# A hybrid two-layer trunk on one core: other buffers, engines and a fixed order for the first chunk

## The chip, the cores and the metric

The kernel runs on one core of one Trainium2 chip. The metric is the device time of one execution in microseconds (us), as the median of several runs of the same program. Five engines work side by side, each through its own list of instructions in order: TensorE (PE; its weight loads are shown apart as PEld), VectorE (DVE), ScalarE (ACT), GpSimd (POOL) and SyncE (SP, which here only starts transfers). They wait for one another through semaphores.

## The reference, cut to what matters

All of it is in float32, for 256 tokens of width 1024. A first layer mixes a state-space scan with gated linear attention, a second one is attention; each starts with an RMS norm and ends with a projection that is added to x.

```python
def rms_norm(x, w):
    x32 = x.astype(jnp.float32)
    y = x32 * lax.rsqrt(jnp.mean(x32 * x32, axis=-1, keepdims=True) + RMS_EPS)
    return y * w.astype(jnp.float32)

def ssd_gla_layer(x, norm_w, w_in, ...):
    h = rms_norm(x, norm_w)
    u = h @ w_in.astype(jnp.float32)
    z_a, xbc, dt_raw, q_b, k_b, v_b, gate_lr, g_b = split_cols(u, EVEN_SPLITS)
    ...
    out = jnp.concatenate([y_a, o_b], axis=-1) @ w_out.astype(jnp.float32)
    return x + out.astype(x.dtype)

def reference(x, ...):
    x = ssd_gla_layer(x, ...)
    x = moba_layer(x, ...)
    return rms_norm(x, final_norm).astype(x.dtype)
```

Only the very first part matters here: x times its norm weights goes into the first products at once, and the sum of squares of x, from which the norm's factor comes, is applied to the products afterwards.

## The kernel before, in words

**Products.** Each float32 operand is split into a high part (`float32r`) and the rest: `h_...` and `l_...` for weights, `hhi` and `hlo` for x. A product is three matmuls (high by high, high by low, low by high: `mm3`, line 158 is the matmul). ScalarE makes a weight's high part (line 78), VectorE the low part (line 79), both in `split`.

**Weight pieces.** Weights come from HBM as a list of pieces, in the order of use: eight pieces of the first token-major chunk (`a0_0` to `a0_7`, 128x416, one for each of the 8 row blocks of x), then `b_8` and `b_9` (128x1024 each, feature-major blocks), then `a1_0` to `a1_3` (128x832), `b_0` and so on. A piece lands in one of the 4 buffers of the pool `wraw`, and such a buffer is free again when its piece has been split. High and low parts have 7 buffers each. `need(piece)` asks for a piece and splits up to four pieces ahead of it.

**The first chunk.** `CUTS_A0` gives the transfers on SP's queue in pairs: row block k of x (`xT`, 128x256, line 186) and piece `a0_k` (line 72). Each block of x is then scaled by its norm weights into `hhi` (even blocks on VectorE, line 214; odd ones on ScalarE, line 212) and `hlo` (VectorE, line 215). TensorE runs 20 warm-up matmuls on zeros (`warmp`, line 176) and then 6 matmuls for each of the 8 blocks into `pa0_0` and `pa0_1`; then come the 24 matmuls of the block `pb8`, of `pb9`, and then of chunk a1.

**The squares of x.** `xsq` is x squared, in four pairs of row blocks: two pairs on GpSimd (line 224), two on ScalarE (line 222). Four additions on GpSimd (line 226) bring the eight blocks down to one. TensorE then sums over the partitions with a matmul on ones (`ss1`), which stands in its list after the 15th matmul of `pb8`. From `ss1` come `rcol_v` (VectorE) and `rcol` (GpSimd, a power), with which all products of the layer are scaled.

**Order.** TensorE's list is written out in program order (`manual_schedule`), with the small products of the mixers put between those of the projections after given delays (`DL`). The lists of the other engines are ordered by the scheduler. SP starts a transfer when the buffer is free and when the transfer that used the same one of 8 transfer semaphores has landed.

Of the kernel before, what the change touches and what calls it, by code (L numbers as in the profile page):

```python
# [9 lines left out]
F32 = mybir.dt.float32  # L10
F32R = mybir.dt.float32r
AF = mybir.ActivationFunctionType
ALU = mybir.AluOpType
AX = mybir.AxisListType

P = 128
T = 256
D = 1024
KB = D // P
# [1 line left out]
NEG = -1e30  # L21
NW = 7
NWARM = 20
# first weight pieces: (first row block, number of them)
CUTS_A0 = tuple((k, 1) for k in range(8))
AHEAD = 4
# tensor-engine time (ns) left to the other engines between the steps of a mixer
DL = {"ss": 1350, "rb": 5000, "gt": 1500, "ac": 7300, "act": 2600, "lg": 2150, "ln": 2250, "cb": 12400,
      "pair0": 11900, "pair1": 9700, "gla0": 650, "glagap": 3650, "gla1": 3350, "gla2": 8700, "r2": 10000,
      "turn": 4150, "rb1": 4000, "at0": 2600, "at2": 4350, "at3": 1800, "gqk": 250}  # L30
# feature-major blocks of the first projection: 0-9 convolved, 10-13 q, 14-17 k, 18-25 gate
# a1-a4: chunks of the token-major columns
ORDER_A = (8, 9, "a1", 0, 10, 1, 11, 2, 14, 3, 13, 5, 12, 4, 15, 16, 6, "a3", 7, 17, "a2", "a4")
GLA_NEEDS = ("a3", "a3", "a4", "a4")

# columns of the packed constants
C_EN, C_SN, C_ON = 0, 8, 16
C_CW, C_CB, C_GB, C_DS, C_GN = 24, 64, 74, 78, 86
C_DTB, C_AL = 87, 103
C_N = 119  # L40
# columns of the packed matrices of shape
M_ID, M_TRI, M_MASK, M_SEL = 0, 128, 384, 768
M_N = 784

# [2 lines left out]
def trunk(ctx, tc, xT_d, x_d, cst_d, mat_d, gw2_d, fn_d, wa_d, wb_d, wc_d, wv_d, wp_d, wf_d, out_d):  # L47
    nc = tc.nc
    V, S, G, TE = nc.vector, nc.scalar, nc.gpsimd, nc.tensor
# [5 lines left out]
    big = ctx.enter_context(tc.tile_pool(name="big", bufs=1))  # L55
# [7 lines left out]
    def pg(name):  # L63
        return psg.tile([P, 512], F32, name=name, tag="g")
# [1 line left out]
    def pm(name):  # L66
        return psm.tile([P, 512], F32, name=name, tag="m")

    # ------------------------------------------------------------------ weights
    def fetch(src, kbs, cols, name):  # L70
        raw = wraw.tile([P, kbs, cols], F32, name="r_" + name, tag="raw")
        nc.sync.dma_start(raw, src)
        return raw

    def split(raw, kbs, cols, name):
        hi = whi.tile([P, kbs, cols], F32R, name="h_" + name, tag="hi")
        lo = wlo.tile([P, kbs, cols], F32R, name="l_" + name, tag="lo")
        S.activation(hi, raw, AF.Copy)  # L78
        V.tensor_sub(lo, raw, hi.bitcast(F32))  # L79
        return hi, lo  # L80

    pieces, index, got, raws = [], {}, [], []
# [5 lines left out]
    def prefetch(end):  # L88
        for j in range(len(got), min(len(pieces), end)):
            k_, src, kbs, cols = pieces[j]  # L90
            name = "_".join(str(q_) for q_ in k_)
            if j >= len(raws):
                raws.append(fetch(src, kbs, cols, name))
            got.append(split(raws[j], kbs, cols, name))

    def need(key, oldest=None):
        i = index[key]
        prefetch(max(i + 1, min(i + AHEAD, index[oldest or key] + NW)))
        return got[i]
# [22 lines left out]
    for n in range(2):  # L122
        plan_tm(f"f{n}", wf_d[n])

    # ------------------------------------------------------------------ order of the tensor engine
    # The projections are the main stream; the mixers are generators that run beside it.
    # A generator yields the tensor-engine time (ns) after which its next step may be queued.
    clock = {"now": 0.0, "seq": 0}
    waiting = []

# [34 lines left out]
    def mm3(ps, ahi, alo, bhi, blo, first, last):  # L165
        mm(ps, ahi, bhi, first, False)
        mm(ps, ahi, blo, False, False)
        mm(ps, alo, bhi, False, last)
        due()

    # keep the tensor engine's clock up until the first operands arrive
    warm = cpool.tile([P, T], F32R, name="warm")
    V.memset(warm.bitcast(F32), 0.0)
    wps = pm("warmp")
    for _ in range(NWARM):
        TE.matmul(wps[:, 0:T], warm[:, 0:P], warm, start=True, stop=True)

    # ------------------------------------------------------------------ inputs
    xT = big.tile([P, KB, T], F32, name="xT", tag="xT")
    cst = cpool.tile([P, C_N], F32, name="cst")  # L180
    mat = cpool.tile([P, M_N], F32, name="mat")
    gw2 = cpool.tile([16, 512], F32, name="gw2")
    nc.scalar.dma_start(cst, cst_d)
    j = 0
    for k0, n_ in CUTS_A0:
        nc.sync.dma_start(xT[:, k0:k0 + n_, :], xT_d[:, k0:k0 + n_, :])
        for k_, src, kbs, cols in pieces[j:j + (1 if j < len(CUTS_A0) - 1 else 3)]:
            raws.append(fetch(src, kbs, cols, "_".join(str(q_) for q_ in k_)))
        j += 1
    nc.sync.dma_start(mat, mat_d)  # L190
    nc.sync.dma_start(gw2, gw2_d)

    ident = mat[:, M_ID:M_ID + P]
# [10 lines left out]
    hhi = big.tile([P, KB, T], F32R, name="hhi", tag="hhi")  # L204
    hlo = big.tile([P, KB, T], F32R, name="hlo", tag="hlo")
    xsq = big.tile([P, KB, T], F32, name="xsq", tag="y")
    kb = 0
    for i, n_ in enumerate(n_ for _, n_ in CUTS_A0):
        for kb in range(kb, kb + n_):
            en = cst[:, C_EN + kb:C_EN + kb + 1]  # L210
            if kb % 2:
                S.activation(hhi[:, kb, :], xT[:, kb, :], AF.Copy, scale=en)
            else:
                V.tensor_scalar(hhi[:, kb, :], xT[:, kb, :], en, None, op0=ALU.mult)
            V.scalar_tensor_tensor(hlo[:, kb, :], xT[:, kb, :], en, hhi[:, kb, :].bitcast(F32),  # L215
                                   op0=ALU.mult, op1=ALU.subtract)
        kb += 1
        prefetch(i + 1)
    for k4 in range(4):
        sq, src = xsq[:, 2 * k4:2 * k4 + 2, :], xT[:, 2 * k4:2 * k4 + 2, :]  # L220
        if k4 % 2:
            S.activation(sq, src, AF.Square)
        else:
            G.tensor_tensor(sq, src, src, op=ALU.mult)
    for a, b, n_ in ((0, 2, 2), (4, 6, 2), (0, 4, 2), (0, 1, 1)):
        G.tensor_tensor(xsq[:, a:a + n_, :], xsq[:, a:a + n_, :], xsq[:, b:b + n_, :], op=ALU.add)

    def rms_from_sum(ss, n, width, name):
        v = sm.tile([P, n], F32, name=name + "_v", tag=name + "_v")
# [18 lines left out]
    rhalf, rsq, rsv, rsh = (cpool.tile([P, 2], F32, name=n_) for n_ in ("rhalf", "rsq", "rsv", "rsh"))  # L248
    env = {}

    # ------------------------------------------------------------------ even in-projection
    v = big.tile([P, 2, D], F32, name="v", tag="v")
    gs = big.tile([P, 2, D], F32, name="gs", tag="gs")
    dtr = sm.tile([P, 2, 16], F32, name="dtr", tag="dtr", bufs=1)
# [17 lines left out]
            V.scalar_tensor_tensor(gs[:, tt, glo:ghi], th[:, 0:n], 1.0, src, op0=ALU.add, op1=ALU.mult)  # L272

    def gemm_tm(name, hi8, lo8, cols, outs, cuts=((0, 2), (2, 2), (4, 2), (6, 2))):
        """Token-major product of both token tiles, a weight piece at a time."""
        for q_, (k0, n_) in enumerate(cuts):
            hi, lo = need((name, k0 if name == "a0" else q_))
            for tt in range(2):
                for j in range(n_):
                    kb = k0 + j  # L280
                    mm3(outs[tt][:, 0:cols], hi8[:, kb, tt * P:tt * P + P], lo8[:, kb, tt * P:tt * P + P],
                        hi[:, j, :], lo[:, j, :], kb == 0, kb == KB - 1)

    def gemm_a(c):
        ps = [pg(f"pa{c}_{tt}") for tt in range(2)]
        cuts = CUTS_A0 if c == 0 else ((0, 2), (2, 2), (4, 2), (6, 2))
        gemm_tm(f"a{c}", hhi, hlo, 416, ps, cuts)
        return ps
# [28 lines left out]
    def co_first(ps):  # L317
# [9 lines left out]
        yield DL["rb"]  # L327
        S.activation(rb, row_bcast([rcol[:, tt:tt + 1] for tt in range(2)], "rbp")[:, 0:T], AF.Copy)
        env["rb"] = True
        # softplus of the step sizes, by the series of artanh  # L330
        V.scalar_tensor_tensor(na, dtr, -1.0, dtr, op0=ALU.mult, op1=ALU.min)
        S.activation(se, na, AF.Exp)
        V.tensor_scalar(sd, se, 2.0, None, op0=ALU.add)
# [25 lines left out]
        for tt in range(2):  # L359
            TE.transpose(act[:, 16 * tt:16 * tt + 16], acT[:, tt * P:tt * P + P], ident[0:16, 0:16])  # L360
        V.tensor_copy(acs, act[:, 0:32].rearrange("p (a b) -> p a b", a=2))
        # gate logits -> cumulated log decay (times 16)
        for b2 in range(2):
            lg = pm(f"lg{b2}")
            for j in range(2):
                b = 2 * b2 + j
                mm(lg[:, j * T:j * T + T], gw2[:, b * P:b * P + P], glT)
            for j in range(2):
                b = 2 * b2 + j
# [8 lines left out]
        V.tensor_tensor_scan(flat(gcs), flat(scanm), flat(gmn), 0.0, op0=ALU.mult, op1=ALU.add)  # L378
        env["gcs"] = True

    # convolution and silu
    xs = big.tile([P, KB, T], F32, name="xs", tag="xT")
    bc = big.tile([P, 2, T], F32, name="bc", tag="bc")
    pads = []
# [68 lines left out]
        V.scalar_tensor_tensor(y[:, blk, :], xs[:, blk, :], cst[:, C_DS + blk:C_DS + blk + 1], yp[:, 0:T],  # L453
                               op0=ALU.mult, op1=ALU.add)

    # gated linear attention
    q = big.tile([P, 4, T], F32, name="q", tag="obhi")
    k = big.tile([P, 4, T], F32, name="k", tag="oblo")
    f3 = lambda a: a.rearrange("p a (c d) -> p (a c) d", d=64)
# [120 lines left out]
            if env["nqk"] == 8:  # L580
                spawn(co_gla_qk())

    # ------------------------------------------------------------------ gate of the state-space half
    x1 = big.tile([P, 2, D], F32, name="x1", tag="xT")
    nc.scalar.dma_start(x1, x_d)
    ylate = {}
# [22 lines left out]
    for b in range(KB):  # L609
# [3 lines left out]
                               op0=ALU.mult, op1=ALU.subtract)  # L613
# [4 lines left out]

    spawn(co_r2())

    # ------------------------------------------------------------------ even out-projection
    for n in range(2):
        ps = [pg(f"pc1_{n}_{tt}") for tt in range(2)]
        gemm_tm(f"c1{n}", obhi, oblo, 512, ps)
# [8 lines left out]
                kb == 0, kb == KB - 1)  # L633

    def gemm_tt(name, hi8, lo8, tag):
        """Token-major product, one token tile after the other: yields each when it is done."""
        for tt in range(2):
            ps = pg(f"{tag}{tt}")
            part(ps, name, hi8, lo8, tt, range(KB), (name, 0) if tt == 0 else None)
            yield tt, ps  # L640
# [39 lines left out]
            due()  # L680
    spawn(co_norm())

    # ------------------------------------------------------------------ second layer
    va = big.tile([P, 2, D], F32, name="va", tag="y")
    for n in range(2):
        for tt, ps in gemm_tt(f"v{n}", h1hi, h1lo, f"pv{n}"):
# [52 lines left out]
    for pr in range(8):  # L739
        qk = []  # L740
        for i in range(2):
            ps = gemm_fm(("p", 3 * pr + i), h1hi, h1lo, f"pp{pr}_{i}")
            t_ = tmp.tile([P, T], F32, name=f"qk{pr}_{i}", tag=("t1a", "t1c")[i])
            n_ = (P, T)[i]
# [18 lines left out]
        V.scalar_tensor_tensor(zs, th, 1.0, zs, op0=ALU.add, op1=ALU.mult)  # L763
        env[("z", pr)] = zs

    # ------------------------------------------------------------------ last projection and norm
    fnb = big.tile([P, D], F32, name="fnb", tag="s2")
    nc.scalar.dma_start(fnb, fn_d.to_broadcast([P, D]))
    ssf = sm.tile([P, 2, 3], F32, name="ssf", tag="ssf", bufs=1)
# [122 lines left out]
```

## Time and profile before

| | before |
|---|---|
| median of 3 runs | 349.83 us |
| fastest and slowest run | 348.47 and 350.31 us |
| span of the profiled execution | 347.5 us |
| PE busy | 335.5 us, 97% |
| DVE, ACT, POOL busy | 263.5, 217.5 and 49.3 us |

The span goes from the first to the last instruction of the profiled execution. The page gives that execution no own time beside its span; the three timed runs lie 1.0 to 2.8 us above the span. PE's busy time is modelled (matmuls overlap), so its pace is read from the distance between starts.

### The profile page before, as it was taken

How to read it: one execution, taken by the hardware profiler on the slowest of the kernel's cores; microseconds unless marked ns; L12 is line 12 of the kernel's file. 1: busy time of each engine (PE TensorE's matmuls, PEld its weight loads, DVE VectorE, ACT ScalarE, POOL GpSimd, SP SyncE). 2: the span in 40 equal slices, each digit the busy share in tenths (PEclk: the TensorE clock that was granted, in tenths of full speed). 3: DMA queues.
4: the chain of work that ended last, by engine and by line, in shares of the span. 5: the costliest groups of instructions: out<-in, count | busy, mean ns of one | idle time of the engine just before them, and what ended most of it. 6: DMA issues, size and time to landing. Idle time of an engine off the chain costs nothing.

```text
span 347.5 us, 6341 instructions
## 1 busy us (share of the span) xinstructions
PE 335.5 (97%) x2352; PEld 305.2 (88%) x2352; DVE 263.5 (76%) x548; ACT 217.5 (63%) x445; POOL 49.3 (14%) x62
## 2 busy tenths in 40 slices
PE   8699999999999999999999999999999999999992
PEld 7599989998999899999888888899999999998792
DVE  5979999999989658789974775377777877777243
ACT  5547689898765757577542676466657665674222
POOL 2610001112415442434200000000000000000000
PEclk9999999999999999999999999999999999999998
DMA  7778672365573745631685634766344335430003
GB/s 209 238 245 283 219 255 94 80 185 178 162 227 115 252 132 170 186 117 41 207 296 189 201 121 163 241 210 214 124 158 146 123 122 183 122 123 0 3 0 121
DMA packets 17631, 56.09 MB, mean 161 GB/s; under 512 B 2096, under 2 KB 4144, under 8 KB 17472
## 3 DMA queue, kind: packets, MB, share of 16 engines
q1 hardware_dynamic: 16880, 53.53, 47.7%
q10 hardware_dynamic: 720, 2.16, 1.8%
q8 instruction: 18, 0.29, 0.4%
q14 instruction: 13, 0.11, 0.1%
HBM read 54.63 MB, written 1.05 MB: 160 GB/s over the span
## 4 chain that ended last, share of the span: by engine, by line
PE 85%; DVE 5%; issue 3%; DMA 2%; POOL 2%; SPq 0%; ACT 0%; POOLq 0%; DVEq 0%
PE pp L158 21%; PE pb L158 18%; PE pc L158 13%; PE pa L158 11%; PE pv L158 6%; PE pf L158 4%; DMA r_a<-in_wa 2%; PE ao L158 2%; PE yp L158 2%; PE as L158 2%; PE ptp L162 2%; PE gs L158 1%; PE go L158 1%; POOL rr L537 1%; POOL sT L517 1%
## 5 line engine op out<-in xcount | busy, mean ns | idle before, releaser
L158 PE MATMUL pb<-hhi,h_b 128*128 128x256 f32 x208 | 60.0, 288 | 0.0
L158 PE MATMUL pb<-hlo,h_b 128*128 128x256 f32 x208 | 58.7, 282 | 0.0
L158 PE MATMUL pb<-hhi,l_b 128*128 128x256 f32 x208 | 58.7, 282 | 0.0
L158 PE MATMUL pp<-h1hi,h_p 128*128 128x256 f32 x192 | 56.3, 293 | 0.0
L158 PE MATMUL pp<-h1lo,h_p 128*128 128x256 f32 x192 | 54.2, 282 | 0.0
L158 PE MATMUL pp<-h1hi,l_p 128*128 128x256 f32 x192 | 54.2, 282 | 0.0
L158 PEld LDWEIGHTS pb<-hhi,h_b 128*128 128x128 f32 x208 | 39.7, 191 | 1.2 <-issue 1.1
L158 PEld LDWEIGHTS pb<-hlo,h_b 128*128 128x128 f32 x208 | 39.7, 191 | 0.0
L158 PEld LDWEIGHTS pb<-hhi,l_b 128*128 128x128 f32 x208 | 39.7, 191 | 0.0
L79 DVE TENSOR_TENSOR l_p<-r_p,h_p 128x1024 fp32r<-128x1024 f32 x24 | 29.4, 1225 | 12.2 <-ACT h_p L78 11.6
L158 PEld LDWEIGHTS pp<-h1hi,h_p 128*128 128x128 f32 x192 | 36.6, 191 | 2.1 <-issue 1.0
L158 PEld LDWEIGHTS pp<-h1lo,h_p 128*128 128x128 f32 x192 | 36.6, 191 | 0.0
L158 PEld LDWEIGHTS pp<-h1hi,l_p 128*128 128x128 f32 x192 | 36.6, 191 | 0.0
L78 ACT ACTIVATE h_b<-r_b 128x1024 fp32r<-128x1024 f32 x26 | 27.4, 1067 | 9.5 <-DMA r_b<-in_wb 5.3
L79 DVE TENSOR_TENSOR l_b<-r_b,h_b 128x1024 fp32r<-128x1024 f32 x26 | 31.3, 1214 | 1.8 <-ACT h_b L78 1.8
L158 PE MATMUL pa<-l_a,hhi 128*128 128x416 f32 x80 | 28.4, 354 | 3.0 <-DVE l_a L79 3.0
L78 ACT ACTIVATE h_p<-r_p 128x1024 fp32r<-128x1024 f32 x24 | 25.3, 1056 | 9.5 <-PE pp L158 5.4
L158 PE MATMUL pa<-h_a,hhi 128*128 128x416 f32 x80 | 29.0, 363 | 0.1
L158 PE MATMUL pa<-h_a,hlo 128*128 128x416 f32 x80 | 28.2, 353 | 1.0 <-DVE hlo L215 1.0
L79 DVE TENSOR_TENSOR l_a<-r_a,h_a 128x832 fp32r<-128x832 f32 (+1 forms) x24 | 22.8, 960 | 2.2 <-ACT h_a L78 2.2
L79 DVE TENSOR_TENSOR l_c<-r_c,h_c 128x1024 fp32r<-128x1024 f32 x16 | 19.9, 1252 | 4.8 <-ACT h_c L78 4.8
L78 ACT ACTIVATE h_c<-r_c 128x1024 fp32r<-128x1024 f32 x16 | 16.9, 1056 | 10.1 <-DMA r_c<-in_wc 6.3
(241 smaller groups left out, 804.4 us busy)
## 6 DMA issues: line engine op xcount, KB each, us to landing
r_b<-in_wb SPq DMA_DIRECT2D x26, 512.0 KB, 4.2
r_p<-in_wp SPq DMA_DIRECT2D x24, 512.0 KB, 4.0
r_c<-in_wc SPq DMA_DIRECT2D x16, 512.0 KB, 4.2
r_a<-in_wa SPq DMA_DIRECT2D x16, 416.0 KB, 3.6
r_v<-in_wv SPq DMA_DIRECT2D x8, 512.0 KB, 4.5
r_f<-in_wf SPq DMA_DIRECT2D x8, 512.0 KB, 3.5
r_a<-in_wa SPq DMA_DIRECT2D x8, 208.0 KB, 3.6
xT<-in_xT SPq DMA_DIRECT2D x8, 128.0 KB, 3.6
```

The source lines that it names most:

```text
L78: S.activation(hi, raw, AF.Copy)
L79: V.tensor_sub(lo, raw, hi.bitcast(F32))
L158: TE.matmul(out, lhsT, rhs, start=start, stop=stop)
L162: TE.transpose(out, in_, ident)
L517: G.affine_select(out=sT[:, 0:3:2, :], in_=sT[:, 0:3:2, :], pattern=[[0, 2], [1, P]], compare_op=ALU.is_ge, fill=0.0, base=0, channel_mult ...
L537: G.tensor_tensor(rr, ss, mhalf, op=ALU.pow)
```

## The change

The eight pieces `a0_k` get buffers of their own: two tiles `first0` and `first1`, which take the places of the later tiles `gs` and `v`. So the pool `wraw` is free for `b_8`, `b_9`, `a1_0` and `a1_1`, whose transfers are now started straight behind (with the matrices `mat` between). The high part of x is made on ScalarE for blocks 1 to 7. All four squares are on ScalarE, all four additions on VectorE. This part of VectorE's and ScalarE's lists is written out by hand, the splits of the pieces up to `b_9` among it. The rest is the same (comments are dropped).

```diff
-    j = 0
-    for k0, n_ in CUTS_A0:
-        nc.sync.dma_start(xT[:, k0:k0 + n_, :], xT_d[:, k0:k0 + n_, :])
-        for k_, src, kbs, cols in pieces[j:j + (1 if j < len(CUTS_A0) - 1 else 3)]:
-            raws.append(fetch(src, kbs, cols, "_".join(str(q_) for q_ in k_)))
-        j += 1
+    first = [big.tile([P, 4, 416], F32, name=f"first{i}", tag=t_) for i, t_ in enumerate(("gs", "v"))]
+    for k_, src, kbs, cols in pieces[0:8]:
+        kb = k_[1]
+        nc.sync.dma_start(xT[:, kb, :], xT_d[:, kb, :])
+        raws.append(first[kb // 4][:, kb % 4:kb % 4 + 1, :])
+        nc.sync.dma_start(raws[-1], src)
+    for k_, src, kbs, cols in pieces[8:10]:
+        raws.append(fetch(src, kbs, cols, "_".join(str(q_) for q_ in k_)))
     nc.sync.dma_start(mat, mat_d)
+    for k_, src, kbs, cols in pieces[10:12]:
+        raws.append(fetch(src, kbs, cols, "_".join(str(q_) for q_ in k_)))
     nc.sync.dma_start(gw2, gw2_d)
...
-    kb = 0
-    for i, n_ in enumerate(n_ for _, n_ in CUTS_A0):
-        for kb in range(kb, kb + n_):
+    with tc.manual_schedule(engines={mybir.EngineType.DVE, mybir.EngineType.Activation}):
+        for kb in range(KB):
             en = cst[:, C_EN + kb:C_EN + kb + 1]
-            if kb % 2:
+            if kb == 0:
+                V.tensor_scalar(hhi[:, kb, :], xT[:, kb, :], en, None, op0=ALU.mult)
+            else:
                 S.activation(hhi[:, kb, :], xT[:, kb, :], AF.Copy, scale=en)
-            else:
-                V.tensor_scalar(hhi[:, kb, :], xT[:, kb, :], en, None, op0=ALU.mult)
             V.scalar_tensor_tensor(hlo[:, kb, :], xT[:, kb, :], en, hhi[:, kb, :].bitcast(F32),
                                    op0=ALU.mult, op1=ALU.subtract)
-        kb += 1
-        prefetch(i + 1)
-    for k4 in range(4):
-        sq, src = xsq[:, 2 * k4:2 * k4 + 2, :], xT[:, 2 * k4:2 * k4 + 2, :]
-        if k4 % 2:
-            S.activation(sq, src, AF.Square)
-        else:
-            G.tensor_tensor(sq, src, src, op=ALU.mult)
-    for a, b, n_ in ((0, 2, 2), (4, 6, 2), (0, 4, 2), (0, 1, 1)):
-        G.tensor_tensor(xsq[:, a:a + n_, :], xsq[:, a:a + n_, :], xsq[:, b:b + n_, :], op=ALU.add)
+            prefetch(kb + 1)
+        prefetch(9)
+        for k4 in range(4):
+            S.activation(xsq[:, 2 * k4:2 * k4 + 2, :], xT[:, 2 * k4:2 * k4 + 2, :], AF.Square)
+            if k4 % 2:
+                a = 2 * k4 - 2
+                V.tensor_tensor(xsq[:, a:a + 2, :], xsq[:, a:a + 2, :], xsq[:, a + 2:a + 4, :], op=ALU.add)
+        prefetch(10)
+        for a, b, n_ in ((0, 4, 2), (0, 1, 1)):
+            V.tensor_tensor(xsq[:, a:a + n_, :], xsq[:, a:a + n_, :], xsq[:, b:b + n_, :], op=ALU.add)
```

**VectorE, from the last piece of the first chunk to the first use of `ss1`, before.** `l_` rows are low parts of pieces (`l_b_8` is that of piece b_8), `sel` is a small copy out of `mat`, `rcol_v` reads `ss1`.

```order
L79 TENSOR_TENSOR l_a0_7_197<-r_a0_7_134,h_a0_7_196 128x416
L79 TENSOR_TENSOR l_b_8_279<-r_b_8_136,h_b_8_278 128x1024
L79 TENSOR_TENSOR l_b_9_289<-r_b_9_138,h_b_9_288 128x1024
L356 CAST sel_231<-mat_109 128x16
L231 TENSOR_SCALAR rcol_v_335<-ss1_332 128x2
```

The same place with the change:

```order
L79 TENSOR_TENSOR l_a0_7_197<-first1_113,h_a0_7_196 128x416
L79 TENSOR_TENSOR l_b_8_201<-r_b_8_130,h_b_8_200 128x1024
L227 TENSOR_TENSOR xsq_149<-xsq_149 128x512
L360 CAST sel_240<-mat_109 128x16
L227 TENSOR_TENSOR xsq_149<-xsq_149 128x512
L79 TENSOR_TENSOR l_b_9_211<-r_b_9_132,h_b_9_210 128x1024
L230 TENSOR_TENSOR xsq_149<-xsq_149 128x512
L79 TENSOR_TENSOR l_a1_0_300<-r_a1_0_135,h_a1_0_299 128x832
L230 TENSOR_TENSOR xsq_149<-xsq_149 128x256
L79 TENSOR_TENSOR l_a1_1_310<-r_a1_1_137,h_a1_1_309 128x832
L235 TENSOR_SCALAR rcol_v_332<-ss1_329 128x2
```

The four additions (L227, L230) now stand in VectorE's list behind the split of b_8, and the last of them behind the splits of b_9 and a1_0 too, which the scheduler put between.

**ScalarE at the same place, before** (`h_` rows are high parts of pieces; `v` is the copy of the products of the first chunk out of `pa0_0` and `pa0_1`):

```order
L222 ACTIVATE xsq_151<-xT_107 128x512
L78 ACTIVATE h_a0_7_196<-r_a0_7_134 128x416
L78 ACTIVATE h_b_8_278<-r_b_8_136 128x1024
L78 ACTIVATE h_b_9_288<-r_b_9_138 128x1024
L78 ACTIVATE h_a1_0_300<-r_a1_0_298 128x832
L265 ACTIVATE v_213<-pa0_0_246,rsq_210 128x384
```

With the change:

```order
L78 ACTIVATE h_a0_7_196<-first1_113 128x416
L78 ACTIVATE h_b_8_200<-r_b_8_130 128x1024
L224 ACTIVATE xsq_149<-xT_107 128x512 x4
L78 ACTIVATE h_b_9_210<-r_b_9_132 128x1024
L78 ACTIVATE h_a1_0_299<-r_a1_0_135 128x832
L78 ACTIVATE h_a1_1_309<-r_a1_1_137 128x832
L78 ACTIVATE h_a1_2_359<-r_a1_2_357 128x832
L78 ACTIVATE h_a1_3_392<-r_a1_3_390 128x832
L269 ACTIVATE v_222<-pa0_0_255,rsq_219 128x384
```

All four squares now stand behind the split of b_8, and the copy `v` behind four splits of a1 in place of one.

TensorE's list holds the same matmuls in the same order before and with the change. Its place that matters here, with the change (before, the same rows stand there):

```order
L158 MATMUL pa0_1_256<-h_a0_7_196,hlo_148 128x416
L158 MATMUL pb8_313<-hhi_147,h_b_8_200 128x256
L158 MATMUL pb8_313<-hlo_148,h_b_8_200 128x256
L158 MATMUL pb8_313<-hhi_147,l_b_8_201 128x256
...
L158 MATMUL pb8_313<-hhi_147,l_b_8_201 128x256
L158 MATMUL ss1_329<-ones_140,xsq_149 128x1 x2
L158 MATMUL pb8_313<-hhi_147,h_b_8_200 128x256
```

`ss1` stayed after the 15th matmul of `pb8`.

## Rows read from the trace of the kernel before

**Rows 1.** The page, part 1: busy us, share of the span, instructions.

```profile
PE 335.5 (97%) x2352; PEld 305.2 (88%) x2352; DVE 263.5 (76%) x548; ACT 217.5 (63%) x445; POOL 49.3 (14%) x62
```

**Rows 2.** PE's longest wait in the whole span: us, times, longest.

```profile
PE pa L158 <- DVE l_a L79: 3.0, 3, 2.0
```

**Rows 3.** Timeline of PE, 1 to 22.5 us: start, us, operation [idle before].

```profile
1.25 4.64 PE L176 MATMUL warmp<-warm 128*128 128x256 f32 x20 [1.25 <-DVE mhalf L199]
5.69 0.55 PE L158 MATMUL pa<-h_a,hhi 128*128 128x416 f32 x1
...
18.17 0.46 PE L158 MATMUL pa<-l_a,hhi 128*128 128x416 f32 x1 [1.99 <-DVE l_a L79]
...
18.66 0.35 PE L158 MATMUL pa<-h_a,hhi 128*128 128x416 f32 x1
...
20.34 0.28 PE L158 MATMUL pb<-hhi,h_b 128*128 128x256 f32 x1
...
22.01 0.28 PE L158 MATMUL pb<-hhi,l_b 128*128 128x256 f32 x1
22.13 0.50 PE L158 MATMUL ss<-ones,xsq 128*128 128x1 f32 x4
```

**Rows 4.** Timeline of POOL and DVE, 9 to 19 us.

```profile
9.78 0.35 DVE L214 TENSOR_SCALAR hhi<-xT,cst 128x256 fp32r<-128x256 f32 x1
...
13.77 3.90 POOL L226 TENSOR_TENSOR xsq<-xsq 128x512 f32<-128x512 f32 x3 [0.65 <-ACT xsq L222]
...
14.23 1.38 DVE L214 TENSOR_SCALAR hhi<-xT,cst 128x256 fp32r<-128x256 f32 x1
...
15.64 1.44 DVE L215 SCALAR_TENSOR_TENSOR hlo<-xT,cst,hhi 128x256 fp32r<-128x256 f32 x1
...
17.01 1.11 DVE L79 TENSOR_TENSOR l_a<-r_a,h_a 128x416 fp32r<-128x416 f32 x1
18.04 0.47 DVE L215 SCALAR_TENSOR_TENSOR hlo<-xT,cst,hhi 128x256 fp32r<-128x256 f32 x1
...
18.44 0.58 DVE L79 TENSOR_TENSOR l_a<-r_a,h_a 128x416 fp32r<-128x416 f32 x1
```

**Rows 5.** Timeline of SP's issues and the first split of b_8.

```profile
9.89 0.33 SPq L72 DMA_DIRECT2D r_a<-in_wa  x1
...
12.02 2.63 SPq L72 DMA_DIRECT2D r_b<-in_wb  x2
...
15.38 1.06 ACT L78 ACTIVATE h_b<-r_b 128x1024 fp32r<-128x1024 f32 x1 [1.31 <-DMA r_b<-in_wb]
```

**Rows 6.** DMA issues from 9.7 to 10 us: KB each, us to landing.

```profile
r_a<-in_wa SPq DMA_DIRECT2D x1, 208.0 KB, 3.2
```

**Rows 7.** Windows: us, busy of PE, PEld, DVE, ACT, POOL; granted clock, DMA share, GB/s.

```profile
4.00:12.00 8.00, 7.02 (x34) 6.16 (x33) 7.06 (x14) 5.13 (x11) 2.54 (x3) 1.00 0.92 277
20.00:22.00 2.00, 2.00 (x17) 2.00 (x16) 1.37 (x3) 0.33 (x1) 0.00 (x0) 1.00 1.00 363
```

**Rows 8.** Timeline of ACT and DVE: operations that the change moves, or like them.

```profile
13.02 0.61 ACT L222 ACTIVATE xsq<-xT 128x512 f32<-128x512 f32 x1
...
13.54 0.54 ACT L78 ACTIVATE h_a<-r_a 128x416 fp32r<-128x416 f32 x1
...
18.94 2.35 DVE L79 TENSOR_TENSOR l_b<-r_b,h_b 128x1024 fp32r<-128x1024 f32 x2
...
21.21 0.16 DVE L356 CAST sel<-mat 128x16 fp32r<-128x16 f32 x1
...
24.70 1.02 DVE L79 TENSOR_TENSOR l_a<-r_a,h_a 128x832 fp32r<-128x832 f32 x1
...
341.93 0.43 DVE L778 TENSOR_TENSOR x<-x,fnb 128x256 f32<-128x256 f32 x1 [0.57 <-ACT jf L775]
```

**Rows 9.** PE's last matmul, from the timeline.

```profile
340.62 0.28 PE L158 MATMUL pflast<-h_f,oglo 128*128 128x256 f32 x1
```

**Rows 10.** Windows of PE at the end: us, busy, granted clock, DMA share, GB/s.

```profile
344.20:344.30 0.10, 0.00 (x0) 0.66 0.00 0
```

## The prediction

> **What bounds the kernel now.** The busy shares come first: PE is busy for 97% of the span [rows 1], so the kernel is as long as TensorE's list plus the places where that list stands still. The list of PE's waits says where that is: its longest entry is the wait for the low parts of weight pieces of chunk `a` [rows 2], and the timeline puts it into the first 20 us. After `pb8` begins, no wait of PE for another engine stands in that list.
>
> The timeline of PE gives the size. From 18.66 to 20.34 nine matmuls of 416 columns begin, one every 0.187 us [rows 3]. The 48 matmuls of the first chunk would so take 8.98 us, and from the first at 5.69 they would be through at 14.67. `pb8` begins at 20.34 [rows 3]. So 5.7 us are lost in the first chunk, and nearly all that any edit of this part could win is there.
>
> Why the pieces are late is seen beside it. From 13.77 to 17.67 GpSimd adds squares; within this stretch VectorE's `hhi` takes 1.38 us, its `hlo` 1.44 and an `l_a` 1.11, where the same operations take 0.35, 0.47 and 0.58 when GpSimd is idle [rows 4]. That is 2.5 us of delay for VectorE in front of the matmul that then waits 1.99 us [rows 3]. The second cause is SP: `b_8` is issued only at 12.02, because its buffer is still in use, and its split waits until 15.38 for the data [rows 5].
>
> **The change part by part.**
>
> *Own buffers.* Before, `a0_7` was issued at 9.89 and landed 3.2 us later, at 13.1 [rows 5, 6]. From 4 to 12 us the DMA engines were busy for 0.92 of the time [rows 7], so the transfers nearly fill them already: a queue that is never empty can win at most 8% of the 9.1 us from 4.0 to 13.1, which is 0.7 us. So `a0_7` lands between 12.4 and 13.1; I take 12.7. `b_8` follows straight behind: 0.524 MB at 363 GB/s [rows 7] are 1.44 us, so it lands at T = 14.1 (13.8 to 14.5), against 15.38 before.
>
> *`hhi` on ScalarE.* Blocks 2, 4 and 6 move from VectorE, three times 0.35 us [rows 4]. ScalarE then has a `hhi` and a piece of 0.54 us [rows 8] for each block; no row above shows its `hhi`, which lies under the 0.54 us of a wider piece. Together that is at most 1.08 us in a block, and a block of 0.344 MB takes 1.24 us to come at the 277 GB/s of 4 to 12 us [rows 7]. ScalarE's waiting for data hides it. If that cover were gone, it would be 0.5 us on the last block, which is less than the next term gives back.
>
> *Squares and sums off GpSimd.* The 2.5 us go, and so does a similar delay at earlier blocks. VectorE needs 0.47 + 0.58 us in a block and keeps up with the transfers. The last block is then ready at 12.7 + 0.54 + 0.58 + 0.1 for signals = 13.9, its last five matmuls take 0.93, and the first chunk ends at 14.9. **That is 5.4 us before the 20.34 of now.** If nothing were late next, this would be the gain.
>
> *What is late next: the split of `b_8`.* High part 1.06 us [rows 5], low part 1.17 (two in 2.35 us [rows 8]), and 0.1 for signals: the third matmul of `pb8` can go at T + 2.35 = 16.45. From there 13 matmuls, one every 0.119 us (15 from 20.34 to 22.01 [rows 3]), lead to `ss1`: TensorE comes there at T + 3.9 = 18.0. Before, it came there at 22.13 [rows 3], and the sums had been ready since 17.67 [rows 4], hidden by 4.5 us. This cover was what made GpSimd's sums free.
>
> *And then: the sums themselves.* Now they stand behind the splits, in the lists shown above. ScalarE: `h_b_8` to T + 1.06, then four squares. One takes 0.61 us, but the next operation began 0.52 after it [rows 8], so they end at T + 3.2, and `h_b_9` at T + 4.2. VectorE: `l_b_8` to T + 2.35; the first addition; `sel` (0.16 [rows 8]); the second addition when the fourth square is there, from T + 3.2. No row shows an addition of 512 columns in SBUF. It is bounded by 0.43 us (256 columns) and 1.02 (832) [rows 8]; nearest is the `l_a` of 416 columns with 0.58 [rows 4], and with 96 columns more I take 0.65. So the second addition ends at T + 3.85. Then `l_b_9`, which waits for `h_b_9`, from T + 4.2 to T + 5.4; the third addition to T + 6.05; `l_a1_0` (1.02, less what overlaps) to T + 7.0; the last addition, 256 columns, 0.43 [rows 8], to T + 7.45. **`ss1` goes at T + 7.5 = 21.6**, and TensorE has waited 3.6 us for it, just behind the stall that was removed. Queued behind the last addition on VectorE are `l_a1_1` and `rcol_v`; behind `ss1` on PE is everything.
>
> *The sum.* `ss1` moves from 22.13 to 21.6: 0.5 us are won. All of TensorE's list behind it is the same, without a wait now [rows 2], so the shift reaches the end as it is: the span goes from 347.5 to 347.0. The median stands 2.3 us above the profiled span, and I carry the shift over: 349.83 - 0.5 = 349.3 us. The bounds: with T = 13.8 and additions of 0.5 us it is 1.3 us won; with T = 14.5 and nothing overlapping on either engine (T + 8.0) 0.4 us lost.
>
> **The rivals.**
>
> *The clock falls in the new wait (slower).* TensorE would stand for 3.6 us before `ss1`. In this trace its last matmul begins at 340.62 [rows 9], and in the window from 344.20 the granted clock is 0.66, on its way from 1.00 to 0.50 [rows 10]; so it fell some 3.6 us after the last start. The wait of 1.99 us [rows 3] did not bring it down: over 4 to 12 and 20 to 22 it stays 1.00 [rows 7]. The new wait is just about as long as the one that did, and it decides from there on. Its price: the 20 warm-up matmuls of 256 columns took 4.44 us to the next start, 0.222 each [rows 3], the pace of 1.2 GHz, against 0.119 at 2.4 GHz. If the low level lasts as long again, 4.4 us, then 4.4 x (1 - 0.119/0.222) = 2.0 us are lost, and the time is 349.3 + 2.0 = 351.3 (up to 352 where the sums are later too, since a longer wait makes it likelier). Chance 0.2. The Trainium skill, "TensorE: Matmul & The Clock Gate", section "Part 1: The HAM clock gate", says that the throttled state is the default and activity releases it, with 1.2 GHz after idling; by that rule the change is a loss of 1.5 us, by the row of the 1.99 us wait alone a gain of 0.5, and the trace agrees with the rule at the end of the kernel only.
>
> *The sums are not late (faster).* If they came before T + 3.9, `ss1` would go at 18.0 and 4.1 us would be won: 345.7 us. For it speaks only that the stall of the first chunk does go. Against it speaks the order: four squares on ScalarE alone reach to T + 3.2, and two splits that need `b_9` and `a1_0` stand before the last addition. Only data much before T = 14.1 would help, and the share of 0.92 leaves no room. Chance 0.1, with the part ways (T near 13, 348) in it.
>
> *Another new wait, in chunk a1.* The copies `v` that free `pa0_0` now stand behind `h_a1_3`. Its transfer cannot start before `l_b_9` has freed a buffer, T + 5.4; with 3.2 to 3.5 us to land [rows 5, 6], some 0.9 to split (between the 0.54 and 1.06 of a narrower and a wider piece [rows 5, 8]) and some 0.6 a copy, it is free at T + 10.4. TensorE needs it 33 matmuls of `pb8` and `pb9` after `ss1`, at T + 11.8. With 1.4 us of room I count it as nothing; a landing 2 us later makes 0.6 us of it, and lists in another order behind it may cost some tenths too: about 350.0. Chance 0.15.
>
> **How the numbers follow.** The forecast has 0.55, at 349.3 us, its own range 348.5 to 350.3. A measurement of this kernel can tell about 0.5% (1.75 us) from no change. Faster by more than that, below 348.1, are the second rival and a little of the forecast's lower tail: 0.14. Slower, above 351.6, is the upper half of the first rival and little else: 0.12. The rest, 0.74, is within 0.5%. For 8 times in 10 the range leaves out most of the second rival and the top of the first: 347.7 to 351.7.
>
> **What would show it.** In the profile of the changed kernel: PE's waits for `l_a` and `hlo` in the first chunk down to a few tenths each, VectorE's operations there at 0.35, 0.47 and 0.58 us; the first chunk's end near 14.9; `b_8` split from 14.1; and in their place one wait of `ss` for VectorE's `xsq` of 3 to 4 us, with `ss` starting near 21.6. The granted clock behind it tells the first rival. I am wrong where `ss` starts near 18 (the order of the sums did not matter), where the first chunk still ends after 17 (then GpSimd or the buffers were not what held it), or where a wait of PE appears after `ss`.

## The result, and the profile after

The changed kernel takes 351.0 us in the median of 20 runs (350.07 to 353.0), the kernel before 349.68 in 20 runs beside it. The ratio is 1.0057, 95% interval 1.0042 to 1.0072: **slower by 0.57%, 2.0 us**, where 0.5 us less was forecast. (The medians alone lie 1.3 us apart, since the times of the kernel before fall into two groups, which the experiment with fillers in it looks at.) The time lies inside the range that was given, but on the other side, and it is the case that had been given a chance of 0.2: the clock.

PE's waits in the profile after (us, times, longest). The waits of the first chunk, 3.0 us for `l_a` in [rows 2], are gone but for 0.2; one of 3.1 us for the sums of squares stands in their place.

```profile
PE ss L158 <- DVE xsq L230: 3.1, 1, 3.1
...
PE pb L158 <- DVE l_b L79: 0.8, 1, 0.8
PE pa L158 <- DVE l_a L79: 0.2, 1, 0.2
```

The timeline of PE answers to [rows 3]. The first chunk now ends at 15.5 and `pb8` begins at 15.69 (20.34 before). `ss1` begins at 21.85 (22.13 before).

```profile
15.30 0.34 PE L158 MATMUL pa<-h_a,hlo 128*128 128x416 f32 x1
15.69 0.39 PE L158 MATMUL pb<-hhi,h_b 128*128 128x256 f32 x1
...
18.48 0.28 PE L158 MATMUL pb<-hhi,l_b 128*128 128x256 f32 x1
21.85 0.94 PE L158 MATMUL ss<-ones,xsq 128*128 128x1 f32 x4 [3.10 <-DVE xsq L230]
...
23.44 0.41 PE L158 MATMUL pb<-hhi,h_b 128*128 128x256 f32 x1
23.65 0.41 PE L158 MATMUL pb<-hlo,h_b 128*128 128x256 f32 x1
...
29.39 0.35 PE L158 MATMUL pa<-h_a,hhi 128*128 128x416 f32 x1
```

After `ss1` the matmuls of 256 columns begin 0.21 us apart (23.44, 23.65), where they were 0.119 apart before. The windows say why (us, PE busy, granted clock, DMA share, GB/s): the clock is at its lower level, 1.2 GHz, for all of 22 to 28 us. A finer window, 21.90 to 22.00 with a granted clock of 0.83, puts its fall at about 21.97: 3.5 us after the start of the last matmul ahead of the wait, and 0.1 us after `ss1` has begun. It rises at some 28.8.

```profile
20.00:22.00 2.00, 0.15 (x1) 0.99 0.52 93
22.00:24.00 2.00, 2.00 (x10) 0.50 0.88 243
24.00:26.00 2.00, 2.00 (x11) 0.50 0.95 352
26.00:28.00 2.00, 2.00 (x11) 0.50 0.78 258
28.00:30.00 2.00, 2.00 (x14) 0.80 1.00 320
```

From `ss1` to chunk a1 TensorE needs 29.39 - 21.85 = 7.5 us; before, it began a1 at 26.53 and had needed 26.53 - 22.13 = 4.4 us for the same. That is 3.1 us lost, 0.3 won by the earlier `ss1`: 2.8 us, which is all of the difference between the spans (350.3 and 347.5). The executions of the changed kernel have mean granted clocks from 0.979 to 0.993; this one has 0.984, and only one of the 20 has less. It took 352.05 us, 1.05 more than the median, so its loss is larger than that of most runs.

VectorE's timeline shows its last two operations on x and on `a0_7`, at 0.48 and 0.59 us again, and the sums where the order of the lists had put them:

```profile
12.12 0.48 DVE L219 SCALAR_TENSOR_TENSOR hlo<-xT,cst,hhi 128x256 fp32r<-128x256 f32 x1
13.79 0.59 DVE L79 TENSOR_TENSOR l_a<-first,h_a 128x416 fp32r<-128x416 f32 x1 [1.19 <-ACT h_a L78]
...
16.82 0.68 DVE L227 TENSOR_TENSOR xsq<-xsq 128x512 f32<-128x512 f32 x1
17.42 0.17 DVE L360 CAST sel<-mat 128x16 fp32r<-128x16 f32 x1
17.75 0.69 DVE L227 TENSOR_TENSOR xsq<-xsq 128x512 f32<-128x512 f32 x1 [0.17 <-ACT xsq L224]
18.70 1.22 DVE L79 TENSOR_TENSOR l_b<-r_b,h_b 128x1024 fp32r<-128x1024 f32 x1 [0.26 <-ACT h_b L78]
19.84 0.68 DVE L230 TENSOR_TENSOR xsq<-xsq 128x512 f32<-128x512 f32 x1
20.45 1.02 DVE L79 TENSOR_TENSOR l_a<-r_a,h_a 128x832 fp32r<-128x832 f32 x1
21.38 0.42 DVE L230 TENSOR_TENSOR xsq<-xsq 128x256 f32<-128x256 f32 x1
```

### The profile page after: what moved, and what is told of

It reads as the page before. It is cut to its first block, busy times and chain, and to the rows that moved or that the text cites. A ratio compares the mean times of both kernels' runs of the same rounds, so it can differ in the third digit from the quotient of the medians.

```text
span 350.3 us, 6332 instructions
## 1 busy us (share of the span) xinstructions
PE 338.3 (97%) x2352; PEld 307.9 (88%) x2352; DVE 260.7 (74%) x549; ACT 220.4 (63%) x450; POOL 42.4 (12%) x56
## 3 DMA queue, kind: packets, MB, share of 16 engines
HBM read 54.63 MB, written 1.05 MB: 159 GB/s over the span
## 4 chain that ended last, share of the span: by engine, by line
PE 84%; DVE 4%; issue 3%; DMA 3%; POOL 2%; ACT 2%; SPq 1%; POOLq 0%; ACTq 0%
PE pp L158 20%; PE pb L158 18%; PE pc L158 12%; PE pa L158 11%; PE pv L158 6%; PE pf L158 4%; PE ao L158 2%; PE yp L158 2%; PE as L158 2%; DMA r_b<-in_wb 2%; PE ptp L162 1%; DMA first<-in_wa 1%; PE gs L158 1%; PE go L158 1%; POOL sT L521 1%
## 5 line engine op out<-in xcount | busy, mean ns | idle before, releaser
L158 PE MATMUL pb<-hhi,h_b 128*128 128x256 f32 x208 | 61.4, 295 | 0.0
L158 PE MATMUL pb<-hhi,l_b 128*128 128x256 f32 x208 | 60.0, 289 | 0.8 <-DVE l_b L79 0.8
L158 PE MATMUL pb<-hlo,h_b 128*128 128x256 f32 x208 | 60.0, 288 | 0.0
L158 PEld LDWEIGHTS pb<-hhi,h_b 128*128 128x128 f32 x208 | 41.1, 197 | 1.6 <-issue 1.1
L158 PEld LDWEIGHTS pb<-hhi,l_b 128*128 128x128 f32 x208 | 41.0, 197 | 1.0 <-DVE l_b L79 1.0
L158 PEld LDWEIGHTS pb<-hlo,h_b 128*128 128x128 f32 x208 | 41.1, 198 | 0.0
L79 DVE TENSOR_TENSOR l_c<-r_c,h_c 128x1024 fp32r<-128x1024 f32 x16 | 19.9, 1252 | 5.2 <-ACT h_c L78 5.2
L446 POOL TENSOR_SCALAR_AFFINE_SELECT e<-e 128x256 f32<-128x256 f32 x16 | 12.1, 779 | 76.8 <-ACT e L444 67.3
```

What stands on the lines that cost most here:

```text
L158: TE.matmul(out, lhsT, rhs, start=start, stop=stop)
L446: G.affine_select(out=e[:, j, 0:3:2, :], in_=e[:, j, 0:3:2, :], pattern=[[0, 2], [1, P]], compare_op=ALU.is_ge, fill=0.0, base=0, channel_ ...
```

## The experiments

**The clock alone.** 20 matmuls on zeros keep TensorE at work during the wait.

```diff
     def co_first(ps):
+        fill = pm("fill")
+        for _ in range(20):
+            TE.matmul(fill[:, 0:T], warm[:, 0:P], warm, start=True, stop=True)
         env["rcol"] = rcol = rms_from_sum(colsum(xsq[:, 0, :], "ss1")[:, 0:2], 2, D, "rcol")
```

> The changed kernel with 20 more matmuls of 256 columns on zeros, into a PSUM tile that nobody reads, just ahead of ss1 in TensorE's list. They run while TensorE waits for the sums, so ss1 should start at the same time as in the changed kernel, near 21.85. Theory (the clock is what turns a small gain into a loss): the granted clock stays 1.00 behind ss1, and the span is 0 to 0.5 us shorter than before (347.0 to 347.5), the ratio to before 0.998 to 1.001. Rival (the wait itself or the order of the lists costs the time): the ratio stays at 1.004 to 1.007 as in the changed kernel.

Measured: 349.72 us, ratio to before 1.0008 (0.999 to 1.0026). Two waits of its PE, the start of the split of `b_8`, and windows as above:

```profile
PE pb L158 <- ACT h_b L78: 0.8, 1, 0.8
...
PE ss L158 <- DVE xsq L230: 0.7, 1, 0.7
```

```profile
15.15 1.06 ACT L78 ACTIVATE h_b<-r_b 128x1024 fp32r<-128x1024 f32 x1 [1.87 <-DMA r_b<-in_wb]
```

```profile
22.00:24.00 2.00, 1.57 (x13) 1.00 0.78 219
24.00:26.00 2.00, 2.00 (x19) 1.00 0.91 326
```

`ss1` is no earlier here, it begins at 22.43, since `b_8` came 0.6 us later in this execution (its split begins at 15.15, in the changed kernel at 14.58). Yet the clock stays at 1.00, and most of the loss is gone: 1.0057 - 1.0008 = 0.5%, 1.7 us. The theory holds for the larger part. Not all runs are free of falls (3 of 12 have a mean clock of 0.991 or 0.992 and over 350.2 us).

What is left of the change is no gain of 0.5 us. Against all runs of the kernel before it is about nothing; but half of those have a lower clock themselves. The 8 runs with fillers that have a mean clock of 0.994 or more take 349.28 to 349.99 us, and the 15 such runs of the kernel before beside them 348.42 to 349.26. So where the clock falls on neither side the change still costs some 1 us, as far as the mean clock can sort the runs.

**The place of the sums.** Only the last two additions move, ahead of the splits of `b_9` and `a1_0`. (In the change the split of `b_9` stands ahead of them by hand, through the `prefetch(10)` that moves here; the scheduler put only that of `a1_0` between them.)

```diff
-        prefetch(10)
         for a, b, n_ in ((0, 4, 2), (0, 1, 1)):
             V.tensor_tensor(xsq[:, a:a + n_, :], xsq[:, a:a + n_, :], xsq[:, b:b + n_, :], op=ALU.add)
+        prefetch(10)
```

> The changed kernel with one edit: the last two additions of the squares stand ahead of the split of b_9 and of a1_0 in VectorE's list. Theory (the sums stand too far back; the long wait for them lets the clock fall): the sums are ready at about 19.4 us, ss1 starts near 19.5 (21.85 in the changed kernel), waits under 1 us, and the granted clock stays 1.00. TensorE then comes to chunk a1 near 23.7, where the copies v behind the split of a1_3 (data at about 24) hold it for 1 to 2 us. In all 0.5 to 2 us faster than before, so 2.5 to 4 us faster than the changed kernel. Rival (the loss lies in the other order of the lists behind ss1, the wait and the clock are side effects): within 0.5 us of the changed kernel, some 1.5 us slower than before.

Measured: 348.09 us, ratio 0.9973 (0.9954 to 0.9992), 0.9 us faster than before. PE's waits:

```profile
PE ss L158 <- DVE xsq L229: 0.9, 1, 0.9
...
PE pa L158 <- ACT v L269: 0.6, 1, 0.6
```

`ss1` begins at 20.08, the clock stays 1.00, and the copies `v` hold chunk a1 for 0.6 us. Moving two small additions turns the loss into a gain, so the loss came from their place, with the wait and the clock that it brought.

**One part of the change at a time.** First the buffers and the order of transfers alone, with the rest as before:

```diff
-    j = 0
-    for k0, n_ in CUTS_A0:
...
+    first = [big.tile([P, 4, 416], F32, name=f"first{i}", tag=t_) for i, t_ in enumerate(("gs", "v"))]
+    for k_, src, kbs, cols in pieces[0:8]:
...
```

> The kernel before with one part of the change: own buffers for the first eight pieces and the new order of transfers. Squares and sums stay on GpSimd, the high parts of x stay on both engines, no order by hand. Theory (VectorE, held up by GpSimd, was the larger cause of the stall in the first chunk): the chunk ends between 18 and 19.5 us (20.3 before, 15.7 in the changed kernel), ss1 is not waited for, 1 to 2 us faster than before. Rival (the buffers were the cause): the chunk ends before 17, over 3 us faster.

Measured: 349.08 us, ratio 0.9997 (0.9976 to 1.0018). Neither expectation came out: the chunk ends at 20.87, no earlier than before, although the high part of `a0_7` is begun at 13.07 (13.54 before). VectorE is held up by GpSimd as in [rows 4], and then the clock falls here too:

```profile
12.38 1.90 DVE L219 SCALAR_TENSOR_TENSOR hlo<-xT,cst,hhi 128x256 fp32r<-128x256 f32 x2
14.21 1.65 DVE L79 TENSOR_TENSOR l_a<-first,h_a 128x416 fp32r<-128x416 f32 x1
```

```profile
13.77 0.34 PE L158 MATMUL pa<-h_a,hhi 128*128 128x416 f32 x1
15.91 0.46 PE L158 MATMUL pa<-l_a,hhi 128*128 128x416 f32 x1 [1.79 <-DVE l_a L79]
...
17.32 0.55 PE L158 MATMUL pa<-h_a,hhi 128*128 128x416 f32 x1
17.68 0.72 PE L158 MATMUL pa<-l_a,hhi 128*128 128x416 f32 x1
```

From 16.6 to 19.9 its matmuls of 416 columns begin some 0.35 us apart in place of 0.187. A pause of 2.1 us from start to start, with one of 1.4 us shortly before, stands ahead of this fall. At the full pace the chunk would have ended near 19.3 here, inside the theory's 18 to 19.5. But a gain in time did not come without a fall either: the four runs with mean clocks of 0.995 to 0.997 take 348.5 to 348.87 us, no less than such runs of the kernel before. Own buffers alone do not help.

Then the other part alone, with the pool's buffers (the block under `manual_schedule` of the change, in the kernel before):

```diff
-    kb = 0
-    for i, n_ in enumerate(n_ for _, n_ in CUTS_A0):
...
+    with tc.manual_schedule(engines={mybir.EngineType.DVE, mybir.EngineType.Activation}):
+        for kb in range(KB):
...
```

> The kernel before with the other part of the change: squares on ScalarE, sums on VectorE, high parts of x on ScalarE, this part of the lists in a fixed order; the first pieces stay in the pool's four buffers. Theory: without GpSimd beside it VectorE frees the buffers early enough, so the first chunk still ends near 16, ss1 still waits 2.5 to 4 us for the sums and starts at 21.8 to 22.5, the clock falls in some executions: 1 to 3 us slower than before, like the changed kernel. Rival (own buffers are needed for the early end): the chunk ends after 17.5, the wait of ss1 is under 2 us, the clock does not fall.

Measured: 351.95 us, ratio 1.0077 (1.0051 to 1.0104), with the same wait as the changed kernel. The first chunk does end early: TensorE waits for the split of `b_8` until 16.98. All 6 runs have mean clocks of 0.984 to 0.993.

```profile
PE ss L158 <- DVE xsq L225: 3.1, 1, 3.1
...
PE pb L158 <- ACT h_b L78: 1.2, 1, 1.2
```

So this part alone makes both the gain in the first chunk and the loss behind it. In the profile the loss is made up otherwise, though: `ss1` begins at 23.15, later than expected and 1.0 us later than before; from there to chunk a1 TensorE needs 6.0 us in place of 4.4, 1.6 of it the clock; and a wait of 0.5 us stands further back. Together that is the 3.1 us by which the span is longer.

**The wait moved to another place.** One number: `ss1` stands later in TensorE's list.

```diff
-DL = {"ss": 1350, "rb": 5000,
+DL = {"ss": 4700, "rb": 5000,
```

> The changed kernel with one number changed: the delay DL of the step ss is 4700 in place of 1350, so that ss1 stands some 28 matmuls later in TensorE's list, in pb9. Theory: ss1 starts at about the same time, 21.9, but TensorE works on pb8 and pb9 until then instead of waiting for 3.1 us, so the clock stays 1.00 there; what depends on ss1 is as late as before, and TensorE waits 1.5 to 2.5 us for the copies v ahead of chunk a1. 0.5 to 1.5 us faster than before. Rival (the wait is only moved, clock included): the clock falls ahead of a1 and the ratio stays over 1.003.

Measured: 351.95 us, ratio 1.0074 (1.0044 to 1.0103). The expectation was wrong and the rival right. `ss1` begins at 22.44. TensorE works through `pb8` and `pb9` at the full clock, but all that hangs on `ss1` is as late as before; it stops for 2.9 us ahead of chunk a1, and the clock falls there (its wait, and windows with PE, PEld, DVE, ACT, POOL ahead of the clock):

```profile
PE pa L158 <- ACT v L269: 2.9, 1, 2.9
```

```profile
24.00:26.00 2.00, 0.00 (x0) 0.00 (x0) 2.00 (x10) 0.73 (x2) 0.00 (x0) 1.00 0.93 348
26.00:28.00 2.00, 1.69 (x5) 1.63 (x6) 1.26 (x4) 2.00 (x5) 0.00 (x0) 0.59 0.92 330
```

**The kernel before, with fillers.** In 18 runs of the kernel before beside these, 9 have a mean granted clock of 0.994 to 0.998 and 348.33 to 348.59 us, 9 have 0.991 to 0.993 and 349.75 to 350.59 us. (In the 31 runs beside the experiments above the two part less sharply: three with 0.993 take 348.83 to 348.86 us.) Were the longer ones those in which the clock fell in the first chunk's waits?

```diff
             hi, lo = need((name, k0 if name == "a0" else q_))
+            if name == "a0" and q_ >= 4:
+                for _ in range(6):
+                    TE.matmul(wps[:, 0:T], warm[:, 0:P], warm, start=True, stop=True)
```

> The kernel before with 6 more matmuls on zeros ahead of each of the blocks 4 to 7 of the first chunk, where TensorE waits for VectorE anyway. In its executions the mean granted clock lies at 0.992 in some and at 0.996 in others, and the former are some 1.5 us longer. Theory (the clock falls in the waits of the first chunk in a part of the executions before too): with the fillers nearly all executions are of the shorter kind, the median is 0.3 to 1.2 us lower (ratio 0.9965 to 0.999). Rival (the two kinds have another cause, as the transfers' pace): the same spread of times, ratio 0.9995 to 1.002.

Measured: 349.98 us, ratio 1.0025 (1.0009 to 1.004). All 12 runs have a clock of 0.994 to 0.998, so the lower kind is gone. But the times did not become the shorter ones, and the ratio is what neither the theory nor the rival had: a new wait stands ahead of chunk a1 (`v`, 0.8 us), since VectorE's list came out in another order (a split of a1 now stands ahead of `rcol_v`, which begins at 23.90 in place of 22.68). The run speaks for the clock as what parts the two kinds, and gives no price for it.

**Early squares.** Two squares stand where ScalarE waits for `a0_7`, two behind its split; the additions follow at once, all ahead of the split of `b_9` (`sq` and `add` are the square and the addition of the change).

```diff
+            if kb == KB - 1:
+                sq(0)
+                sq(1)
+                add(0, 2, 2)
             prefetch(kb + 1)
+        sq(2)
+        sq(3)
+        add(4, 6, 2)
         prefetch(9)
-        for k4 in range(4):
...
+        add(0, 4, 2)
+        add(0, 1, 1)
         prefetch(10)
```

> The changed kernel with the squares in places where ScalarE waits for data (two behind the high part of the last block of x, two behind the split of a0_7) and the additions on VectorE as early as their squares allow, the last two straight behind the split of b_8. Theory (only the sums were late; everything else of the change is worth what the first chunk shows): ss1 is not waited for, it starts at 18.5 to 19.5 us (21.85 in the changed kernel, 22.13 before), the clock stays 1.00; chunk a1 then waits up to 1 us for the copies v. 2 to 3.3 us faster than before, ratio 0.990 to 0.994. Rival (a later wait, for the copies v or the data of a1, takes back what ss1 gains): ratio 0.996 to 0.999, like the run in which only the two last additions were moved.

Measured: 346.24 us, ratio 0.9915 (0.9891 to 0.994). `ss1` begins at 19.21 without a wait. With `tc.high_priority()` around the steps from `ss1` to the copies `v` besides:

```diff
     def co_first(ps):
-        env["rcol"] = rcol = rms_from_sum(colsum(xsq[:, 0, :], "ss1")[:, 0:2], 2, D, "rcol")
+        with tc.high_priority():
+            env["rcol"] = rcol = rms_from_sum(colsum(xsq[:, 0, :], "ss1")[:, 0:2], 2, D, "rcol")
...
```

> As the kernel with the early squares, and the steps from ss1 to the copies v with priority, so that on ScalarE v stands ahead of the splits of a1_2 and a1_3, and on VectorE rcol_v ahead of that of a1_0. Theory: the wait for v ahead of chunk a1 goes, up to 1 us faster than the kernel with the early squares alone, ratio to before 0.988 to 0.993. Rival (TensorE is held ahead of a1 by the data of a1_0, or not at all): within 0.3 us of it.

Measured: 345.96 us, ratio 0.9912 (0.9889 to 0.9935): no different from the one without, as the rival had it. `ss1` begins at 19.05. PE's waits and the windows in which the changed kernel had the low clock:

```profile
PE pb L158 <- DVE l_b L79: 0.8, 1, 0.8
PE pa L158 <- DVE l_a L79: 0.3, 1, 0.3
```

```profile
20.00:22.00 2.00, 2.00 (x19) 1.00 0.77 193
22.00:24.00 2.00, 2.00 (x17) 1.00 0.82 270
```

Last, this kernel with the buffers and transfers of before:

```diff
-    first = [big.tile([P, 4, 416], F32, name=f"first{i}", tag=t_) for i, t_ in enumerate(("gs", "v"))]
...
+    j = 0
+    for k0, n_ in CUTS_A0:
...
```

> The kernel with the early squares and the early steps from ss1, but with the first eight pieces in the pool's four buffers and the transfers in the order of before. Theory (own buffers are a small part: without GpSimd beside it VectorE frees the pool's buffers early enough): the split of b_8 begins some 0.8 us later than with own buffers (15.9 against 15.05), ss1 starts near 19.9 (19.05 with own buffers), no long wait, the clock stays: 0.5 to 1.2 us slower than with own buffers, ratio to before 0.993 to 0.996. Rival (own buffers carry the gain): ss1 after 21, ratio 0.998 or more.

Measured: 346.8 us, ratio 0.9927 (0.9905 to 0.9949), `ss1` at 19.66 with a wait of 0.3 us. The own buffers are worth 0.6 us of `ss1` in the profiles; in the times the two intervals overlap.

## Why the prediction was wrong, by its steps

*GpSimd holds VectorE up, and that makes the first chunk late: right.* After the change VectorE's operations there take 0.48 and 0.59 us, and the chunk ends 4.8 us earlier (15.5; 14.9 was forecast). With own buffers alone the chunk is not early; without GpSimd it is. That second run also moves high parts of x to ScalarE and fixes the order by hand, and no run parts these three; that GpSimd is the cause among them is read from the durations of VectorE's operations beside it.

*Transfers: forecast too early.* A queue that is never empty raised the rate more than allowed for (277 to 315 GB/s from 4 to 12 us, where 8% was to be the most), and yet `a0_7` landed at 13.1, as before (12.7 forecast): it was issued at 8.23 in place of 9.89 and took 4.9 us in place of 3.2. The split of `b_8` began at 14.58, where the text had T = 14.1 and the bounds 13.8 to 14.5. In the five profiles with own buffers in which that split waited for its data it began between 14.58 and 15.19. The last section says where the bytes went.

*The sums stand too far back: right, by row.* `ss1` at 21.85 (21.6 forecast), the additions of 512 columns at 0.68 us (0.65), the idle of PE 3.1 us (3.6). Taking the two additions forward gave 0.9 us against before, and taking the squares forward too gave 3.0 us. The copies `v` made no wait in the changed kernel, as was counted; they made one of 0.6 us where only the two additions had moved.

*The step that failed is the weighing of the first rival, which left the price of the clock at nothing in the sum.* The text put the new wait at 3.6 us, read from the end of the trace that the clock had fallen 3.6 us after the start of a last matmul, and still gave the fall 0.2, because the wait of 1.99 us "did not bring it down". What the runs showed in its place: behind a wait of 3.1 us the clock fell to half and stayed there for 6.8 us, which cost 3.1 us in the profile, and the mean clock is 0.993 or less in each of 20 runs; with the wait filled 1.7 us came back. The row of the 1.99 us was one execution. In half of the runs of the kernel before the clock is lower, and in the profile of the buffers alone it fell behind pauses of 1.4 and 2.1 us. The chance belonged above one half, and the forecast with it on the slower side.

*Its price was too small for the profiled execution, about right for the median.* 2.0 us had been worked out from 4.4 us at the low level. In the profiled execution the level stayed low for 6.8 us. Over the runs the fillers bring 1.7 us back. That the 351.3 us given for this case lie so near the measured 351.0 is partly luck, since the 0.5 us won that stand in them did not come.

*The sum without the clock was wrong too: 0.5 us won were forecast, and T is the term that was mis-sized.* From the start of the split of `b_8` to `ss1` it took 7.3 us in the changed kernel (14.58 to 21.85) and with the fillers (15.15 to 22.43), near the 7.5 of the text. But with T at 14.58 to 15.15 in place of 14.1 `ss1` comes between 0.3 us before and 0.3 us after the 22.13 of the kernel before. The fillers put the rest of the change at 0.08% lost, to within 0.2%, against all runs of the kernel before, and at some 1 us lost against those with a high mean clock. The profiles show 0.4 us of that (spans of 347.9 and 347.5); where the remainder lies stays open. One bound was also added up wrongly: T = 13.8 and additions of 0.5 us make 1.0 us won by the text's own terms, not 1.3.

## What to carry to other kernels

Where a stall is removed, the chain that it had covered is next, and so its place in each engine's list has to be worked out along with the gain: here 1.1 us of additions, behind two splits of later pieces, made TensorE wait 3.1 us. A wait of TensorE has two prices, its length and the lower clock behind it; work that fills the wait shows which of the two counts. A single execution in which a pause did not bring the clock down is weak evidence that the next will not either: several runs, with their clocks, are needed for that.

## What the runs showed of the hardware that had not been expected

The clock fell behind pauses of different length, and in the four profiles that show a fall in this stretch TensorE had already been at work again for 0.1 to 0.9 us: in the changed kernel at 21.97, 3.5 us after the last start and 0.1 us after `ss1` had begun; with the buffers alone at about 16.5, behind pauses of 1.4 and 2.1 us (start to start) and 0.6 us after the second had ended. The profile of the kernel before has pauses of 1.1, 1.4 and 2.4 us in the same stretch and keeps a clock of 1.00. So the length of a pause did not by itself tell whether the clock would fall. It stayed low for 6.8 us in the changed kernel and for some 3.4 us with the buffers alone, with TensorE at work throughout. What decides this is not settled by these runs.

More transfers in the queue raised the rate and did not bring the last piece of the first chunk sooner in this execution. These windows of the changed kernel (us, busy of PE, PEld, DVE, ACT, POOL; clock, DMA share, GB/s) answer to [rows 7]:

```profile
0.00:4.00 4.00, 2.75 (x13) 2.75 (x14) 0.36 (x4) 1.35 (x2) 1.53 (x9) 1.00 0.46 128
4.00:12.00 8.00, 7.82 (x41) 7.12 (x41) 6.95 (x16) 6.80 (x15) 0.00 (x0) 1.00 0.99 315
12.00:14.00 2.00, 2.00 (x12) 1.99 (x11) 0.81 (x3) 0.55 (x1) 0.00 (x0) 1.00 0.97 359
```

```profile
13.20 0.55 ACT L78 ACTIVATE h_a<-first 128x416 fp32r<-128x416 f32 x1 [1.22 <-DMA first<-in_wa]
14.58 1.06 ACT L78 ACTIVATE h_b<-r_b 128x1024 fp32r<-128x1024 f32 x1 [0.83 <-DMA r_b<-in_wb]
```

By 13.2 us they had moved 0.51 + 2.52 + 0.43 = 3.5 MB. All up to `a0_7` is 2.75 MB, and the constants, which come through another queue, are 0.06. So some 0.6 MB of later transfers, by this estimate, had been moved before `a0_7`, issued ahead of them, had landed: in this execution transfers of one queue overlapped, and the later ones took a part of the higher rate. `mat`, in the middle of them, took 7.2 us from issue to landing in place of 4.3. With the fillers, where the same transfers stand in the queue, the split of `a0_7` began at 12.73 and that of `b_8` at 15.15, so the share of each piece differs from one execution to the next.
